# A hybrid attention, delta-rule and linear-attention trunk: the scan's chain gets PSUM banks of its own, and a step's output is normed and gated behind the next step

## The chip, the cores and the metric

The kernel runs on one core of a Trainium2 chip. The metric is the device time of one execution in microseconds (us), as the median of several runs. The engines are TensorE (PE: matmuls, and transposes as matmuls with an identity; PEld is its weight load), VectorE (DVE), ScalarE (ACT), GpSimd (POOL) and SyncE (SP), which issues the DMAs. Each engine works through its instructions in a fixed order. The matmuls' results land in PSUM, which the kernel divides into banks of 128 x 512 float32.

## The reference

Two layers of one trunk over 768 tokens (256 context, 512 latent), model width 1024. In a layer one input projection feeds three groups of heads, whose outputs go through one output projection; a gated ConvFFN follows. Norms and modulation stand around both halves. The core of the first half:

```python
parts = split(norm_and_modulate(x) @ w_in)
mla = softmax((q_nope @ k_nope.T + q_rope @ k_rope.T) * scale) @ v     # 8 heads
# gated delta rule, forward and reversed, 4 heads, chunks of 64 tokens:
v_new = u_ - w_ @ S                      # u_ = Tinv @ (v*beta), w_ = Tinv @ (k*beta*exp(gc))
o     = (q*exp(gc)) @ S + A @ v_new
S     = S * glast + kend.T @ v_new
gdn   = headnorm(o_forward + o_reversed) * gate
gla   = gated linear attention, both directions, headnorm, gate       # 4 heads, chunks of 16 in the reference
x     = x + g * norm(concat(mla, gdn, gla) @ w_out)
x     = x + g * norm(ffn(norm_and_modulate(x)))
```

Only `v_new` and the update of `S` are a chain from chunk to chunk; `o` and everything behind it hang off that chain. All values are float32; large products are made of three fp32r matmuls each (high and low halves).

## The kernel before

The kernel is written with a tile framework. A scheduler fixes each engine's order ahead of time from the order of the program, the tiles that are free and its own estimate of times; on the chip each engine then follows its list. PSUM is one pool: a tag `bb` with two tiles of two banks each, and four tags `a`, `b`, `c`, `d` with one bank and one tile each. `self.ab(tags)` takes the next tag of a string by turns (`"bc"`: b, c, b, c), or of `self.tags` when no string is given. A tag's tiles are handed out in program order: a tile that is asked for later waits until all readers of the tag's tile before it are done.

In a layer, `project_in` makes the input projection: the delta rule's part first, then its preparation for each chunk pair (`gdn_prep`), then `gdn_scan`. The rest of the projection (`rest`) is a generator; `pace` takes 8 pieces of it at two places of each scan step (`SN = (8, 8)`), so that its matmuls stand beside the chain. Behind the scan come `mla_project` (K and Q projections in `bb`, and then six V tiles of 128 x 512, each six matmuls into an `ab()` tile and one ACT copy, L1302), attention for the first of four head pairs, `gla()`, attention for the other three pairs (tags `"ab"`), and the output projection w_out from `mh`, `ml`, the split mixed heads. Attention's tile (128 queries, one head pair): scores in `bb`, L1364 maximum, L1367 exponential into P, transposes of P (bank from `ab()`), copies PT (L1381, L1379), products with V, and L1392, one per tile. Its pool A2 takes the place of the pool A1 in which the K, Q and V projections keep their inputs.

The scan has 12 steps; step n works on chunk n forwards and on a mirrored chunk in reverse, with the two directions on the two halves of the partitions. Before the change a step does, in this order:

- `ks` (tags bc): k·S in columns 0 to 255 and q·S in 256 to 511, 8 matmuls (16 rows in the trace)
- L983 and L984 (DVE): r = v - k·S·eg; then `vp` (bc): tt·r; L995 (DVE): vs, its scaled copy
- `up` twice (bc), one per direction: ktok·vs; POOL L1005 scales the state Sb; L1009 (DVE, four) adds up
- L1013 (DVE): tq = q·S·eg, read from ks; POOL adds the stored output of the other direction (L1015); ACT copies vn
- `op` (bc): at·vn; L1028 (DVE): tq + op, or L1025 into the store `ost` where the other direction comes later
- for n where both directions are there: `head_out`: ACT square (L1058), DVE sum (L1059), square root and reciprocal (L243, L244), POOL scale (L1062), two transposes (L215) into a bc bank, two DVE products with the gate (L1069). Behind every second one a DMA writes the gated output (L1051).

In layer 1 the first four steps need no output (context tokens are dropped there).

Of the kernel before, what the change touches and what calls it, by code (L numbers as in the profile page):

```python
# [11 lines left out]
F32 = mybir.dt.float32  # L12
# [3 lines left out]
ALU = mybir.AluOpType  # L16
# [119 lines left out]
class Net:  # L136
# [40 lines left out]
    def s1(self, pool=None):  # L177
        return (pool or self.B).tile([128, 256], F32, name=self.nm("s"), tag="s", bufs=4 if pool is None else 6)
# [132 lines left out]
    def layer(self, l, later):  # L311
# [32 lines left out]

        with self.ahead(HA):
            self.attention(A2, range(EP[l]))
# [208 lines left out]
    def project_in(self, later):  # L555
# [151 lines left out]
        self.tags = "ad"  # L707
# [249 lines left out]
    def gdn_scan(self):  # L957
# [3 lines left out]
        ost = {}  # L961
# [3 lines left out]
        def s1():  # L965
            return self.s1(self.C)

        for n in range(12):
# [3 lines left out]
            ks = self.ab("bc")  # L972
            for y in range(2 if need_o else 1):
                for d in range(2):
                    c = ch[d]
                    for x in range(2):
                        self.mm(ks[half[d], y * 256 + x * 128:y * 256 + x * 128 + 128],
                                self.KQ[c // 2][:, x, y, half[d]], Sb[:, d, x], True, True)
# [7 lines left out]
            vp = self.ab("bc")  # L986

            for h in range(4):
                for d in range(2):
# [6 lines left out]
                                    self.eks[:, n].unsqueeze(2).to_broadcast(b4), op=ALU.mult)  # L996
            for d in range(2):
                t, hf = ch[d] // 2, ch[d] % 2
                up = self.ab("bc")
# [10 lines left out]
            if need_o:  # L1010
                m = (3 if n < 4 else 15) - n
                vn, tq = s1(), s1()
                nc.vector.tensor_tensor(tq.rearrange(h4, h=4), ks[:, 256:].rearrange(h4, h=4), eg, op=ALU.mult)  # L1013
                if m < n:
                    nc.gpsimd.tensor_tensor(tq, tq, ost[m], op=ALU.add)  # L1015
                nc.scalar.copy(vn, vp[:, :256])
                op = self.ab("bc")
                for h in range(4):
                    for d in range(2):
                        e = d * 4 + h  # L1020
                        self.mm(op[half[d], h * 64:(h + 1) * 64], self.AT[ch[d] // 2][half[d], e * 64:(e + 1) * 64],
                                vn[half[d], h * 64:(h + 1) * 64], True, True)
                if m > n:
                    ost[n] = self.C.tile([128, 256], F32, name=self.nm("ost"), tag="ost", bufs=4)
                    nc.vector.tensor_tensor(ost[n], tq, op[:, :256], op=ALU.add)  # L1025
                    continue

                nc.vector.tensor_tensor(tq, tq, op[:, :256], op=ALU.add)  # L1028
                if n % 2 == 0:
                    lo = min(n, m) - 1  # L1030
                    pieces = [(lo * 64, lo * 64 + 256)] if n < 10 else [(256, 384), (640, 768)]
                    zt = self.gates(0, pieces)
                first = (4 if n >= 10 else lo) if n % 2 == 0 else first
                pos = [c - first if c - first < 4 else c - first - 4 for c in (n, m)]
                self.head_out(tq, zt, [64 * pos[(hf - n) % 2] for hf in range(2)], 0)
                if n % 2:
                    self.ungates(zt, 0, pieces)
# [16 lines left out]
    def head_out(self, o, zt, cols, i):  # L1054
# [8 lines left out]
        ps = self.ab("cd" if i else "bc")  # L1063
# [488 lines left out]
```

## Time and profile before

| | |
|---|---|
| median of 3 runs | 2293.04 us (2292.76 to 2298.89) |
| the profiled execution | 2289.3 us, of them 2287.5 in the span |
| PE busy | 2048.7 us, 90% |
| DVE, ACT, POOL busy | 1306.7 (57%), 1013.0 (44%), 532.2 us (23%) |
| mean granted PE clock | 0.932 of full speed |

Busy times are sums over instructions; a PE at 90% over the span can stand still in one stretch and be full in another. Times in rows count from the span's start. A row's idle time in brackets is how long its engine had nothing to do just ahead of it, with the instruction that ended the wait.

### The profile page before, as it was taken

How to read it: one execution, taken by the hardware profiler on the slowest of the kernel's cores; microseconds unless marked ns; L12 is line 12 of the kernel's file. 1: busy time of each engine (PE TensorE's matmuls, PEld its weight loads, DVE VectorE, ACT ScalarE, POOL GpSimd, SP SyncE). 2: the span in 40 equal slices, each digit the busy share in tenths (PEclk: the TensorE clock that was granted, in tenths of full speed). 3: DMA queues.
4: the chain of work that ended last, by engine and by line, in shares of the span. 5: the costliest groups of instructions: out<-in, count | busy, mean ns of one | idle time of the engine just before them, and what ended most of it. 6: DMA issues, size and time to landing. Idle time of an engine off the chain costs nothing. (4 is left out here: it accounts for less than half of the span.)

```text
span 2287.5 us, 44608 instructions
## 1 busy us (share of the span) xinstructions
PE 2048.7 (90%) x18168; PEld 1674.6 (73%) x18168; DVE 1306.7 (57%) x2474; ACT 1013.0 (44%) x1931; POOL 532.2 (23%) x897
## 2 busy tenths in 40 slices
PE   6899999888888799999999978899878777999996
PEld 3677877665667578888888767787656667888886
DVE  3454535668745743354454685555767757655556
ACT  4653323565454633332232556534456346543333
POOL 1442121135402310001010245222122513211102
PEclk8899999998889899999999978999988888999997
DMA  7233345422043354521222332122412042332332
GB/s 261 66 118 102 107 152 163 139 65 72 8 150 94 125 173 161 166 102 56 65 65 67 99 111 83 51 63 93 151 36 96 6 170 95 110 100 93 101 93 92
DMA packets 121998, 235.64 MB, mean 103 GB/s; under 512 B 9088, under 2 KB 74048, under 8 KB 121792
## 3 DMA queue, kind: packets, MB, share of 16 engines
q1 hardware_dynamic: 121792, 232.78, 31.0%
q8 instruction: 143, 2.34, 0.4%
q14 instruction: 63, 0.52, 0.1%
HBM read 204.04 MB, written 28.70 MB: 102 GB/s over the span
## 5 line engine op out<-in xcount | busy, mean ns | idle before, releaser
L212 PE MATMUL bb<-hh,wl 128*128 128x512 f32 (+1 forms) x1520 | 549.9, 362 | 17.8 <-DVE wl L192 8.4
L212 PE MATMUL bb<-hl,wh 128*128 128x512 f32 (+1 forms) x1520 | 545.8, 359 | 8.1 <-POOL hl L552 6.3
L192 DVE TENSOR_TENSOR wl<-wr,wh 128x512 fp32r<-128x512 f32 (+2 forms) x452 | 336.7, 747 | 365.6 <-ACT wh L191 364.1
L212 PE MATMUL bb<-hh,wh 128*128 128x512 f32 (+1 forms) x1520 | 541.5, 356 | 1.6 <-issue 1.6
L191 ACT CAST wh<-wr 128x512 fp32r<-128x512 f32 (+2 forms) x452 | 274.4, 612 | 525.1 <-PE bb L212 366.2
L212 PEld LDWEIGHTS bb<-hh,wl 128*128 128x128 f32 x1520 | 294.5, 194 | 74.5 <-DVE wl L192 11.7
L212 PEld LDWEIGHTS bb<-hl,wh 128*128 128x128 f32 x1520 | 294.6, 194 | 53.8 <-POOL hl L552 10.5
L212 PEld LDWEIGHTS bb<-hh,wh 128*128 128x128 f32 x1520 | 294.5, 194 | 41.4 <-issue 4.1
L212 PE MATMUL bb<-g,wh 128*128 128x512 f32 (+1 forms) x1024 | 263.6, 349 | 2.3 <-DVE g L192 2.3
L1428 POOL TENSOR_SCALAR y<-u,fmt 128x512 f32<-128x512 f32 (+2 forms) x88 | 80.7, 917 | 528.2 <-ACT u L811 526.7
L212 PEld LDWEIGHTS bb<-g,wh 128*128 128x128 f32 x1024 | 181.6, 195 | 27.5 <-DVE g L192 3.3
L212 PE MATMUL bb<-g,wl 128*128 128x512 f32 (+1 forms) x512 | 180.3, 354 | 21.5 <-DVE wl L192 8.5
L212 PEld LDWEIGHTS bb<-g,wl 128*128 128x128 f32 x512 | 99.3, 195 | 37.0 <-ACT g L191 9.3
L811 ACT ACTIVATE u<-bb,fmt 128x512 f32<-128x512 f32 (+1 forms) x118 | 69.0, 613 | 85.7 <-PE bb L212 85.7
L212 PE MATMUL bb<-mh,wl 128*128 128x256 f32 (+1 forms) x256 | 85.4, 334 | 23.1 <-DVE wl L192 15.5
L1455 DVE TENSOR_TENSOR y<-y,bb 128x512 f32<-128x512 f32 (+2 forms) x80 | 54.7, 685 | 82.4 <-PE bb L212 82.1
L507 POOL TENSOR_TENSOR acc<-acc,sq 128x256 f32<-128x256 f32 (+1 forms) x48 | 49.4, 1029 | 187.6 <-ACT sq L505 186.9
L1429 DVE SCALAR_TENSOR_TENSOR y<-u,fmt,y 128x512 f32<-128x512 f32 (+2 forms) x88 | 72.3, 821 | 29.9 <-POOL y L1428 29.9
L212 PE MATMUL bb<-ml,wh 128*128 128x256 f32 (+1 forms) x256 | 84.1, 328 | 0.3
L1367 ACT ACTIVATE P<-bb,ast,srq 128x768 f32<-128x768 f32 (+1 forms) x80 | 72.6, 908 | 25.4 <-DVE ast L1365 15.6
L212 PE MATMUL bb<-mh,wh 128*128 128x256 f32 (+1 forms) x256 | 82.9, 324 | 0.0
L1364 DVE TENSOR_REDUCE ast<-bb 128x1 f32<-128x768 f32 (+1 forms) x80 | 67.3, 843 | 19.3 <-PE bb L212 18.8
(509 smaller groups left out, 3670.6 us busy)
## 6 DMA issues: line engine op xcount, KB each, us to landing
wr<-in_ffn_w_in SPq DMA_DIRECT2D x92, 512.0 KB, 3.5
wr<-in_w_ada SPq DMA_DIRECT2D x80, 512.0 KB, 4.2
wr<-in_ffn_w_out SPq DMA_DIRECT2D x48, 512.0 KB, 3.5
wr<-in_w_in SPq DMA_DIRECT2D x40, 512.0 KB, 4.0
wr<-in_w_out SPq DMA_DIRECT2D x32, 512.0 KB, 3.6
aw<-in_w_ada SPq DMA_DIRECT2D x16, 512.0 KB, 8.9
x<-in_xT SPq DMA_DIRECT2D x16, 384.0 KB, 8.2
wr<-in_w_uq SPq DMA_DIRECT2D x16, 192.0 KB, 2.5
```

Source lines behind the costliest of these rows:

```text
L191: self.nc.scalar.copy(hi, src)
L192: (eng or self.nc.vector).tensor_tensor(lo, src, hi.bitcast(F32), op=ALU.subtract)
L212: self.nc.tensor.matmul(out, l, r, start=start, stop=stop)
L507: (nc.vector, nc.gpsimd)[k % 2].tensor_tensor(acc[k % 2], acc[k % 2], sq, op=ALU.add)
L811: nc.scalar.activation(u[:, a + o:b + o], ps[:, off + a:off + b], AF.Identity, bias=bias)
L1364: nc.vector.reduce_max(st[:, 0:1], sc, axis=AX)
L1367: nc.scalar.activation(P[:, :w], sc, AF.Exp, bias=st[:, 0:1], scale=self.srq[:, t:t + 1], accum_out=st[:, 1:2])
L1428: nc.gpsimd.tensor_scalar(yv, u[:, lo + 1:lo + 1 + n], cw[1], self.fm(P_FCB + i), op0=ALU.mult, op1=ALU.add)
L1429: nc.vector.scalar_tensor_tensor(yv, u[:, lo:lo + n], cw[0], yv, op0=ALU.mult, op1=ALU.add)
L1455: nc.vector.tensor_tensor(y, y, p, op=ALU.add)
```

## The change

The scan's tags become fixed: `ks` takes b and holds k·S alone, `op` takes d and holds q·S in its upper columns and at·vn in the lower, `vp` takes c, `up` takes b and c. The heads' transposes take a. So that a belongs to what is no part of the chain, the fill of `project_in` and everything behind it until attention takes `"a"` alone instead of `"ad"`; attention sets `"ad"` again. L1013 (tq) now reads `op` behind at·vn; the POOL add of `ost` comes behind the DVE add. `head_out` and the DMA behind it are collected in `late` and emitted behind the next step's output. The pool of [128, 256] tiles `s` in the scan has 8 instead of 6.

```diff
--- before.py
+++ after.py
@@ -175,7 +175,7 @@
         return self.B.tile([128, 512], F32, name=self.nm("h"), tag="h", bufs=HB)
 
     def s1(self, pool=None):
-        return (pool or self.B).tile([128, 256], F32, name=self.nm("s"), tag="s", bufs=4 if pool is None else 6)
+        return (pool or self.B).tile([128, 256], F32, name=self.nm("s"), tag="s", bufs=4 if pool is None else 8)
 
     def bb(self):
         return self.ps.tile([128, 1024], F32, name=self.nm("bb"), tag="bb", bufs=2)
@@ -342,6 +342,7 @@
         self.close(A1p)
         A2p, A2 = self.pool("A2")
 
+        self.tags = "ad"
         with self.ahead(HA):
             self.attention(A2, range(EP[l]))
         with self.ahead(HG):
@@ -704,7 +705,7 @@
         for g in before:
             drain(g)
         self.fill = [rest]
-        self.tags = "ad"
+        self.tags = "a"
         self.gdn_scan()
         self.fill = []
         drain(rest)
@@ -965,17 +966,29 @@
         def s1():
             return self.s1(self.C)
 
+        late = []
+
+        def output(n, tq, zt, cols, last):
+            def go():
+                self.head_out(tq, zt[0], cols, 0)
+                if last:
+                    self.ungates(*zt)
+            return go
+
         for n in range(12):
             ch = (n, self.rstep(n))
             need_o = not (last and n < 4)
             half = [slice(64 * (c % 2), 64 * (c % 2) + 64) for c in ch]
-            ks = self.ab("bc")
-            for y in range(2 if need_o else 1):
-                for d in range(2):
-                    c = ch[d]
-                    for x in range(2):
-                        self.mm(ks[half[d], y * 256 + x * 128:y * 256 + x * 128 + 128],
-                                self.KQ[c // 2][:, x, y, half[d]], Sb[:, d, x], True, True)
+
+            ks = self.ab("b")
+            op = self.ab("d") if need_o else None
+            for y, z in ((0, ks), (1, op)):
+                if z is None:
+                    continue
+                for x in range(2):
+                    for d in range(2):
+                        self.mm(z[half[d], y * 256 + x * 128:y * 256 + x * 128 + 128],
+                                self.KQ[ch[d] // 2][:, x, y, half[d]], Sb[:, d, x], True, True)
             eg = self.egs[:, n].unsqueeze(2).to_broadcast(b4)
             r, v = s1(), s1()
             for d in range(2):
@@ -983,7 +996,7 @@
             nc.vector.tensor_tensor(r.rearrange(h4, h=4), ks[:, :256].rearrange(h4, h=4), eg, op=ALU.mult)
             nc.vector.tensor_tensor(r, v, r, op=ALU.subtract)
             self.pace(SN[0])
-            vp = self.ab("bc")
+            vp = self.ab("c")
 
             for h in range(4):
                 for d in range(2):
@@ -994,9 +1007,12 @@
             vs = s1()
             nc.vector.tensor_tensor(vs.rearrange(h4, h=4), vp[:, :256].rearrange(h4, h=4),
                                     self.eks[:, n].unsqueeze(2).to_broadcast(b4), op=ALU.mult)
+            if need_o:
+                vn, tq = s1(), s1()
+                nc.scalar.copy(vn, vp[:, :256])
             for d in range(2):
                 t, hf = ch[d] // 2, ch[d] % 2
-                up = self.ab("bc")
+                up = self.ab("bc"[d])
                 for h in range(4):
                     x, h2 = h // 2, h % 2
                     self.mm(up[64 * h2:64 * h2 + 64, x * 64:x * 64 + 64], self.ktok[half[d], t, h * 64:(h + 1) * 64],
@@ -1009,32 +1025,32 @@
                     nc.vector.tensor_tensor(o, o, up[ps, :128].rearrange("p (x j) -> p x j", x=2), op=ALU.add)
             if need_o:
                 m = (3 if n < 4 else 15) - n
-                vn, tq = s1(), s1()
-                nc.vector.tensor_tensor(tq.rearrange(h4, h=4), ks[:, 256:].rearrange(h4, h=4), eg, op=ALU.mult)
-                if m < n:
-                    nc.gpsimd.tensor_tensor(tq, tq, ost[m], op=ALU.add)
-                nc.scalar.copy(vn, vp[:, :256])
-                op = self.ab("bc")
                 for h in range(4):
                     for d in range(2):
                         e = d * 4 + h
                         self.mm(op[half[d], h * 64:(h + 1) * 64], self.AT[ch[d] // 2][half[d], e * 64:(e + 1) * 64],
                                 vn[half[d], h * 64:(h + 1) * 64], True, True)
+                nc.vector.tensor_tensor(tq.rearrange(h4, h=4), op[:, 256:].rearrange(h4, h=4), eg, op=ALU.mult)
                 if m > n:
                     ost[n] = self.C.tile([128, 256], F32, name=self.nm("ost"), tag="ost", bufs=4)
                     nc.vector.tensor_tensor(ost[n], tq, op[:, :256], op=ALU.add)
-                    continue
-
-                nc.vector.tensor_tensor(tq, tq, op[:, :256], op=ALU.add)
+                else:
+
+                    nc.vector.tensor_tensor(tq, tq, op[:, :256], op=ALU.add)
+                    nc.gpsimd.tensor_tensor(tq, tq, ost[m], op=ALU.add)
+            for go in late:
+                go()
+            late = []
+            if need_o and m < n:
                 if n % 2 == 0:
                     lo = min(n, m) - 1
                     pieces = [(lo * 64, lo * 64 + 256)] if n < 10 else [(256, 384), (640, 768)]
-                    zt = self.gates(0, pieces)
-                first = (4 if n >= 10 else lo) if n % 2 == 0 else first
+                    zt = (self.gates(0, pieces), 0, pieces)
+                    first = 4 if n >= 10 else lo
                 pos = [c - first if c - first < 4 else c - first - 4 for c in (n, m)]
-                self.head_out(tq, zt, [64 * pos[(hf - n) % 2] for hf in range(2)], 0)
-                if n % 2:
-                    self.ungates(zt, 0, pieces)
+                late.append(output(n, tq, zt, [64 * pos[(hf - n) % 2] for hf in range(2)], n % 2))
+        for go in late:
+            go()
 
     def gates(self, i, pieces):
 
@@ -1060,7 +1076,7 @@
         self.rsqrt(ss, ss, 1.0 / 64, self.eps[:, 0:1])
         ov = o.rearrange("p (h j) -> p h j", h=4)
         nc.gpsimd.tensor_tensor(ov, ov, ss.unsqueeze(2).to_broadcast([128, 4, 64]), op=ALU.mult)
-        ps = self.ab("cd" if i else "bc")
+        ps = self.ab("cd" if i else "a")
         for x in range(2):
             self.transpose(ps[:, x * 128:(x + 1) * 128], o[:, x * 128:(x + 1) * 128])
         pv = ps[:, :256].rearrange("p (x c) -> p x c", x=2)
```

How the orders differ. Names end in the number of the tile.

PE, layer 1, the scan's last steps, before: `c_16817` is vp, `b_16828` ks, `d_17627` and `a_17647` are attention's transposes, `bb_17701` its scores.

```order
L212 MATMUL c_16817<-s_16813,at_15545 64x64
L212 MATMUL c_16817<-s_16813,at_15896 64x64
L212 MATMUL b_16828<-Sb_16220,kq_15884 64x128 x2
L212 MATMUL b_16828<-Sb_16220,kq_15533 64x128 x2
L212 MATMUL b_16828<-Sb_16220,kq_15884 64x128 x2
L212 MATMUL b_16828<-Sb_16220,kq_15533 64x128 x2
L215 MATMUL d_17627<-cst,P_17615 128x128 x2
L215 MATMUL a_17647<-cst,P_17641 128x128 x4
L212 MATMUL bb_17701<-K_2871_17442,Q01l_17463 128x512
L212 MATMUL bb_17701<-K_2871_17442,Q01l_17463 128x256
```

In the place of one head pair's tile there now stands the next step; after, in the place of the step that follows vp `c_16972` (`a_16951` are the transposes of a head, `b_16986` and `c_16994` up, `d_16957` op):

```order
L212 MATMUL c_16972<-s_16966,tt_15498 64x64
L212 MATMUL c_16972<-s_16966,tt_15148 64x64
L215 MATMUL a_16951<-cst,s_16856 128x128 x2
L212 MATMUL b_16986<-s_16981,ktok_13578 64x64 x4
L212 MATMUL c_16994<-s_16981,ktok_13578 64x64 x4
L212 MATMUL d_16957<-s_16983,at_15195 64x64
L212 MATMUL d_16957<-s_16983,at_14842 64x64
```

Attention's rows have gone from between the steps; from step 6 to 11 PE has nothing but the scan's own matmuls and the heads' transposes.

PE, layer 1, V, before: `d_17476` and `a_17485` are the first two V tiles, `c_16683` and `b_16691` one step's up.

```order
L212 MATMUL bb_17561<-K_2871_17442,Q01h_17462 128x256
L212 MATMUL d_17476<-wh_17468,kvl_17138 128x512
L212 MATMUL a_17485<-wh_17468,kvl_17138 128x512
L212 MATMUL c_16683<-s_16681,ktok_13578 64x64 x4
L212 MATMUL b_16691<-s_16681,ktok_13578 64x64 x4
L212 MATMUL d_17476<-wl_17469,kvh_17136 128x512
L212 MATMUL d_17476<-wh_17468,kvh_17136 128x512
L212 MATMUL d_17476<-wh_17472,kvl_17139 128x512
L212 MATMUL a_17485<-wl_17469,kvh_17136 128x512
```

After: `d_17030` is the last step's op, `a_17093` and `a_17105` are the last two heads' transposes, `a_17476` and `a_17485` the first two V tiles.

```order
L212 MATMUL d_17030<-s_17056,at_15195 64x64
L212 MATMUL d_17030<-s_17056,at_14842 64x64
L215 MATMUL a_17093<-cst,s_16984 128x128 x2
L215 MATMUL a_17105<-cst,s_17057 128x128 x2
L212 MATMUL a_17476<-wh_17468,kvl_17138 128x512
L212 MATMUL a_17476<-wl_17469,kvh_17136 128x512
L212 MATMUL a_17476<-wh_17468,kvh_17136 128x512
L212 MATMUL a_17476<-wh_17472,kvl_17139 128x512
L212 MATMUL a_17476<-wl_17473,kvh_17137 128x512
L212 MATMUL a_17476<-wh_17472,kvh_17137 128x512
```

The V tiles, which stood among the scan's steps 6 and 7 in two banks by turns, now stand behind the scan and its last head, in one bank.

PE, layer 0, one of the scan's last three steps, before: `a_5115` and `d_5124` are V tiles, `b_4465` and `c_4473` the step's up.

```order
L212 MATMUL a_5115<-wl_5085,kvh_4677 128x512
L212 MATMUL a_5115<-wh_5084,kvh_4677 128x512
L212 MATMUL b_4465<-s_4463,ktok_453 64x64 x4
L212 MATMUL c_4473<-s_4463,ktok_453 64x64 x4
L212 MATMUL d_5124<-wh_5080,kvl_4678 128x512
L212 MATMUL d_5124<-wl_5081,kvh_4676 128x512
```

After, the last step of layer 0: `bb_5027` is the last Q projection, `b_4599` and `c_4607` are up, `d_4570` is op.

```order
L212 MATMUL bb_5027<-cql_4675,wh_5023 128x256
L212 MATMUL bb_5027<-cqh_4672,wh_5023 128x256
L212 MATMUL b_4599<-s_4594,ktok_453 64x64 x4
L212 MATMUL c_4607<-s_4594,ktok_453 64x64 x4
L212 MATMUL d_4570<-s_4596,at_2146 64x64
L212 MATMUL d_4570<-s_4596,at_1788 64x64
```

The last steps have moved ahead of V and attention's transposes, to the end of the Q projections.

## Rows read from the trace of the kernel before

**Rows 1.** The page: span, and busy time, share and instructions of TensorE.
```profile
span 2287.5 us, 44608 instructions
...
PE 2048.7 (90%) x18168; PEld 1674.6 (73%) x18168; DVE 1306.7 (57%) x2474; ACT 1013.0 (44%) x1931; POOL 532.2 (23%) x897
```

**Rows 2.** Busy us of each engine by stretch, granted clock, DMA share, GB/s.
```profile
254.00:437.00 183.00, 171.81 (x1903) 139.58 (x1904) 89.89 (x206) 61.31 (x120) 33.00 (x40) 0.96 0.46 146
...
437.00:492.00 55.00, 44.40 (x389) 33.73 (x388) 37.42 (x97) 39.80 (x75) 12.43 (x25) 0.91 0.20 61
...
1541.00:1632.00 91.00, 83.64 (x1113) 66.27 (x1104) 58.51 (x120) 34.47 (x68) 19.17 (x26) 0.96 0.43 140
...
1632.00:1646.00 14.00, 12.81 (x120) 9.39 (x119) 6.78 (x18) 7.70 (x15) 1.39 (x2) 1.00 0.24 88
...
1692.00:1718.00 26.00, 15.90 (x167) 11.71 (x166) 10.24 (x33) 10.11 (x19) 5.27 (x8) 0.61 0.04 14
...
1718.00:1758.00 40.00, 36.55 (x350) 27.88 (x350) 27.69 (x74) 26.33 (x57) 9.41 (x23) 0.95 0.40 136
...
1758.00:1823.00 65.00, 51.99 (x608) 39.68 (x608) 50.75 (x102) 27.10 (x52) 36.85 (x42) 0.82 0.02 5
...
1823.00:1846.00 23.00, 10.74 (x137) 6.54 (x137) 9.07 (x29) 7.81 (x20) 2.45 (x4) 0.82 0.19 61
```

**Rows 3.** L995 (DVE, one per scan step) by stretch: busy, count, clock.
```profile
437.00:492.00 55.00, 0.84 (x2) 0.91 0.20 61
...
1541.00:1632.00 91.00, 2.52 (x6) 0.96 0.43 140
...
1692.00:1718.00 26.00, 0.85 (x2) 0.61 0.04 14
```

**Rows 4.** Timeline 1698 to 1709: start, us, engine, instruction, count, [idle before <-releaser].
```profile
1698.30 1.12 PE L212 MATMUL c<-s,tt 64*64 64x64 f32 x16 [0.67 <-DVE zt L1069]
...
1699.46 0.42 DVE L995 TENSOR_TENSOR s<-c,eks 128x256 f32<-128x256 f32 x1 [1.30 <-PE c L212]
...
1700.27 0.37 PE L212 MATMUL b<-s,ktok 64*64 64x64 f32 x2 [0.85 <-DVE s L1013]
...
1701.69 0.59 DVE L1009 TENSOR_TENSOR Sb<-Sb,c 64x128 f32<-64x128 f32 x2
...
1703.51 2.03 PE L212 MATMUL b<-Sb,kq 128*64 128x128 f32 x16 [0.58 <-DVE s L1028]
...
1706.03 0.47 DVE L984 TENSOR_TENSOR s<-s,s 128x256 f32<-128x256 f32 x1
...
1707.03 0.69 PE L215 MATMUL c<-cst,s 128*128 128x128 f32 x2 [1.50 <-POOL s L1062]
...
1708.39 1.12 PE L212 MATMUL c<-s,tt 64*64 64x64 f32 x16 [0.67 <-DVE zt L1069]
```

**Rows 5.** Timeline, PE at 1637: the same products at full clock.
```profile
1637.12 1.15 PE L212 MATMUL b<-Sb,kq 128*64 128x128 f32 x16
```

**Rows 6.** Timeline, ACT, 1644 to 1648: last V copy, table, first P.
```profile
1644.81 0.69 ACT L1302 ACTIVATE V<-a,rr 128x512 f32<-128x512 f32 x1 [0.62 <-PE a L212]
...
1645.51 1.28 ACT L1367 ACT_TABLE_LOAD   x1
...
1646.81 0.99 ACT L1367 ACTIVATE P<-bb,ast,srq 128x768 f32<-128x768 f32 x1
```

**Rows 7.** Timeline, PE: GLA's first transposes, w_out's first matmul.
```profile
1742.97 0.44 PE L215 MATMUL c<-cst,h 128*128 128x128 f32 x2
...
1845.47 0.58 PE L212 MATMUL bb<-mh,wl 128*128 128x256 f32 x1 [6.46 <-ACT mh L191]
```

**Rows 8.** L1392 (DVE, one per attention tile) by stretch.
```profile
437.00:492.00 55.00, 1.44 (x5) 0.91 0.20 61
...
1718.00:1758.00 40.00, 1.42 (x5) 0.95 0.40 136
...
1758.00:1823.00 65.00, 1.69 (x6) 0.82 0.02 5
```

## The prediction

> **What bounds the kernel now.** I read the page first, then busy times by stretch, then a timeline of the barest place of the scan, then waits. TensorE (PE) is busy 2048.7 of 2287.5 us [rows 1], so a change that only reorders work can gain no more than the PE's idle time in the two stretches that it touches. Those are layer 0 from 254 to about 655 us and layer 1 from 1541 to w_out's first matmul at 1845.47 [rows 2, 7]; the orders of before and after are the same on every engine elsewhere. Within them the idle lies unevenly. In 254:437 the scan runs beside the rest of the input projection and the K and Q projections, and PE is busy 171.81 of 183 us; in 1541:1632 it is 83.64 of 91. So ten of twelve scan steps in layer 0 (the other two stand in 437:492) and six in layer 1 [rows 3] are well covered, and a shorter chain there gives at most 11 and 7 us. The weak places are later: in 1692:1718 PE is busy 15.90 of 26 us at a granted clock of 0.61, and in 1823:1846 it is 10.74 of 23 [rows 2]. The first holds the last two scan steps [rows 3], with next to no attention beside them; the second holds the end of GLA, and w_out waits there 6.46 us for the split of the last head's output [rows 7].
>
> **What a step costs, before.** The two last steps show it without cover [rows 4]. From one vp to the next (tt times r, which gives the new values) it is 1708.39 - 1698.30 = 10.1 us at low clock. After vp comes L995 (ends 1699.88); up waits for L1013, the DVE instruction that scales the q part of the bank which up takes over (1700.27, idle 0.85); the state is added up by 1702.28; then ks doesn't start, because the attention-matrix product (at times vn) and its reader L1028 come first in the two shared banks; it starts at 1703.51, after 0.58 of waiting for L1028. ks runs to 1705.54, L984 to 1706.50. vp could follow at about 1706.6, but its bank belongs to the head's transposes, which wait 1.50 us for POOL (L1062), and to their reader L1069: 1708.39. So the shared banks cost 0.34 + 1.2 + 1.8 = 3.4 us of the 10.1.
>
> **The change, part by part.** *Banks.* k·S goes to b and q·S to d with at·vn, so up waits for L995 alone and ks for the state alone. Then vp to up is 1.12 + 0.04 + 0.42 + 0.06 = 1.64; up to ks is 1702.28 - 1700.27 + 0.06 = 2.07; ks to vp is 3.1 in the rows (1703.51 to 1706.6). Of its ks, only the k half (1.0 of 2.03 us) must be done before L983, so 2.1. The sum is 5.8 us at low clock, and by the ratio 1.15 to 2.03 of the same ks [rows 4, 5] about 1 us less at full clock. at·vn and the q half fall into the waits for DVE. I take 5.5. Bounds: 4.6, and 8 if the head's DVE and POOL instructions, which stand in the same queues, cut in as often as now.
> *Late output.* The twelve heads' instructions are the same; each is issued a step later. It costs nothing where a next step covers it; behind the last step nothing does. L1059, L1062 (1.50 wait seen by PE), two transposes and L1069 are then bare: from L1028's end, just ahead of ks, to vp's start behind L1069, 1708.39 - 1703.45, about 5 us [rows 4]; I take 5, and 6 with the copy of the last tile.
> *More s tiles, the add of ost behind the DVE add.* No instruction is added. Eight tiles instead of six only free a wait; the POOL add moves between at·vn and the head, off the chain: 0 (bound: one POOL add per step, inside those 5 us).
> *Tags.* This is the part that moves work. project_in's fill, the heads' transposes and the V tiles all take bank a alone, and tiles of one bank are served in program order. V's six tiles are emitted behind the scan, so they cannot start before the last head's transposes. Before, V alternated d and a and could pass the scan's last steps. And attention's first P waits for V's copies (its pool lies where the projection's tiles lay): before, the last V copy ended at 1645.50 and P starts at 1646.81, after the 1.3 us in which ACT loads its table [rows 6]. So attention can't start before the scan is over. The order shows just that: six steps directly behind each other in layer 1, then two heads' transposes, then V.
>
> **Layer 1, summed.** Step 5's vp I put at 1633, as before, where its L995 is the last of six ahead of 1632 [rows 3]: nothing ahead of it moves by more than the 7 idle us of that stretch. Six steps and the rest of this one: 6.6 x 5.5 = 36, to 1669. The last head: 5 to 6, to 1675. V: in d and a by turns the six tiles and one step's work fit into the 14 us of 1632:1646, 12.81 of them busy [rows 2], so a tile has 1.6 us of PE (without the step's 3.0) to 2.3; in one bank each also shows its copy, 0.69 [rows 6], and two starts, so 14 to 20, taken 17: 1692. Table load and P, 1.3 + 0.99 and their starts: 1695, where before had 1648 [rows 6]. From here attention has PE to itself. A tile's pace: five tiles in the 40 us of 1718:1758 [rows 2, 8] is 8.0 us, with GLA's loads and first matmuls already in it, so 7.6 to 8.0, taken 7.8; w_out starts beside the last tile, so 15.7 tiles are 122 us. GLA's own price: before, 1718 to 1846 held 11 tiles [rows 2, 8], 128 - 11 x 8.0 = 40 is the upper bound; the lower is from PE's work alone, 36.55 + 51.99 + 10.74 = 99.3 less 11 x 7.3 (36.55 / 5) = 19. I take 30: GLA starts as soon as the scan has ended (its first transposes stood at 1742.97 [rows 7], 35 us behind the scan's last vp, and will stand beside V) and so mixes with all of attention, but not perfectly. 1695 + 122 + 30 = 1847, against 1845.5: **+1.5**, with -11 (7.6 and 19) and +14 (8.0 and 40) as bounds. In words: the bare 26 us and the tail of 23 us are given back, and a start of attention that is 47 us later is paid for it.
>
> **Layer 0, summed.** Three of the twelve steps stood beside V and attention (two of them in 437:492 [rows 3]); now they come ahead. Of PE's work a step has ks 1.15, vp and at·vn 0.64 each (1.12 by the clock's ratio) and up about 0.5: 3.0 us, so +9 in a stretch where PE idles only 11.2 of 183 us [rows 2]. V in one bank +5, the last head +4, P's start +1.5, and +2 where the fill waits in bank a behind a head's transposes: 21.5. Given back: 437:492 held 5 tiles' ends [rows 8] and two steps in 55 us; without the steps 55 - 5 x 8 = 15 at most, the steps' PE work of 9 at least, taken 11. And of the 11.2 idle us, 7 by a chain that waits less. **+3.5**, bounds -4 and +12.
>
> The sum is +5 on the profiled execution's 2289.3 us. The median of the runs is 2293.04, 3.7 above it, and the runs spread over 6; between 2294 and 2298 I say **2296 us**. That is 0.13% over the median, inside the 0.3% (6.9 us) that a measurement can tell from no change.
>
> **What the rules say.** The six V tiles took d and a in turn and PE was busy 12.81 of 14 us with them and one step [rows 2]. The Trainium skill (Perfetto Trace Analysis, Matmuls) says that independent groups should rotate through different PSUM banks, so that one's evacuation lies beside the next one's matmuls. By that rule alone this part of the change loses some 4 to 6 us in each layer, an estimate, which is what the rows gave above; no row of before has V in one bank. And in 1692:1718 the granted clock is 0.61, between its levels of 1.2 and 2.4 GHz, in the stretch in which PE waits most [rows 2]. The same skill (TensorE: Matmul & The Clock Gate, HAM oscillation) says that idle gaps which come back in each round of a loop throttle the engine again and again. This is the rival C below.
>
> **Rivals.** *B, faster (0.28).* GLA and attention overlap well: PE-bound pace 7.3 and a price of 19 give 1695 + 115 + 19 = 1829, -16; layer 0 with +2 makes -14: about 2279. For it: GLA ends as the very last now, with 12.3 idle us in 23, and starts some 50 us earlier relative to attention after. Against it: in 1758:1823, where both were at work, PE was busy only 51.99 of 65 at clock 0.82 [rows 2].
> *C, slower (0.25).* The bare steps don't shrink: the norm's chain over ACT, DVE and POOL cuts into the chain of the state, and PE waits at low clock as now. At 8 us a step layer 1 loses 6.6 x 2.5 = 16 more; with layer 0's +6 it comes to about +23: 2316. It decides from 6.5 us a step on (+7 us). For it: six such steps in a row instead of two, at 0.61. Against it: three waits in [rows 4] go by construction.
> *D, no effect (0.07).* The cover hides both: PE is busy 94% of 254:437, and in layer 1 the order is overruled by GLA's chain: 2293.
>
> **Chances.** The forecast has 0.40, its own range 2288 to 2304; D is in it. Faster: B 0.28 and 0.03 of the forecast's edge, 0.31. Slower: C 0.25 and 0.09 of the upper edge, 0.34. Same: 0.35. The range takes in B and most of C: 2272 to 2316.
>
> **What would show it.** In layer 1's timeline after: six vp at 5 to 6 us from each other (right) or at 8 and more (C); V's copies all behind the last head's transposes, in one bank, some 2.5 to 3 us apart; the first P near 1695; GLA's last transposes before the last attention tile's end; w_out near 1847 with no 6 us idle ahead. In layer 0, no scan instruction among attention's, and w_out some 3 us later. Wrong would be a first P before 1680 or after 1705, or attention tiles at over 9 us with GLA's work spread among them.

## The result, and the profile after

The changed kernel took 2313.9 us (median of 6 runs, 2308.15 to 2322.89) against 2292.9 for the kernel before (6 runs, 2287.19 to 2298.89): a ratio of 1.0099, with a 95% interval of 1.0076 to 1.0122. It is slower by about 1%. Its profiled execution took 2308.7 us, 19.4 above that of before.

The page of the kernel after, its span and TensorE's row, which answer to [rows 1]:

```profile
span 2307.0 us, 44590 instructions
...
PE 2056.0 (89%) x18168; PEld 1674.4 (73%) x18168; DVE 1314.4 (57%) x2474; ACT 1008.1 (44%) x1927; POOL 534.9 (23%) x897
```

PE's busy time rose by 7 us, the span by 19.5. Four points in each trace part the span: the first step's vs (L995, after L1008), w_out's last matmul in layer 0, a matmul b<-kq of layer 1's preparation of the scan (at 1501.9 before, at 1517.3 after), and w_out's last in layer 1. All times are us; starts of instructions:

| | before | after | difference |
|---|---|---|---|
| first vs | 265.6 | 265.9 | |
| layer 0: to w_out's last matmul | 479.5 | 494.1 | +14.6 |
| between: to layer 1's preparation (nearly the same order) | 756.7 | 757.4 | +0.7 |
| layer 1: to w_out's last matmul | 407.1 | 408.7 | +1.6 |

The loss is layer 0's. Layer 1 came out nearly even, as forecast. Busy us by stretch after (columns as in [rows 2]):

```profile
254.00:436.00 182.00, 172.30 (x1933) 136.24 (x1932) 90.03 (x212) 55.89 (x115) 36.03 (x46) 0.95 0.42 135
...
436.00:472.50 36.50, 24.08 (x104) 15.03 (x103) 15.19 (x39) 10.84 (x24) 8.85 (x15) 0.63 0.36 122
...
472.50:683.00 210.50, 179.49 (x1722) 135.73 (x1722) 152.07 (x367) 128.06 (x260) 79.04 (x110) 0.90 0.21 73
...
1651.00:1683.00 32.00, 24.30 (x399) 17.83 (x399) 22.52 (x65) 9.71 (x25) 10.79 (x17) 0.95 0.04 12
...
1683.00:1690.20 7.20, 2.25 (x30) 1.31 (x28) 3.88 (x14) 1.24 (x4) 1.91 (x3) 0.75 0.11 36
...
1690.20:1714.50 24.30, 13.97 (x54) 9.04 (x54) 2.38 (x7) 7.44 (x15) 2.21 (x6) 0.79 0.26 82
```

The first stretch ends with the last Q projection (before: 420.3), the second with attention's first transposes (before: 436.8), the third with the last attention tile (before: 660.4). The 36.5 us of the second had 16.5 before; PE is busy 24.08 of them, at a granted clock of 0.63. In layer 1 the six bare steps take 1651:1683, then the last heads and V another 31.5 us.

One bare step after, timeline, which answers to [rows 4]:

```profile
1670.84 0.68 PE L212 MATMUL c<-s,tt 64*64 64x64 f32 x16 [0.41 <-DVE s L997]
...
1671.57 0.42 DVE L1008 TENSOR_TENSOR s<-c,eks 128x256 f32<-128x256 f32 x1 [0.78 <-PE c L212]
...
1672.05 0.45 PE L212 MATMUL b<-s,ktok 64*64 64x64 f32 x8 [0.53 <-DVE s L1008]
...
1673.23 0.58 DVE L1025 TENSOR_TENSOR Sb<-Sb,c 64x128 f32<-64x128 f32 x2
...
1673.96 0.62 PE L212 MATMUL b<-Sb,kq 128*64 128x128 f32 x6 [0.18 <-DVE Sb L1025]
...
1674.84 0.42 DVE L996 TENSOR_TENSOR s<-b,egs 128x256 f32<-128x256 f32 x1
...
1675.29 0.78 DVE L997 TENSOR_TENSOR s<-s,s 128x256 f32<-128x256 f32 x1
...
1676.13 0.68 PE L212 MATMUL c<-s,tt 64*64 64x64 f32 x16 [0.40 <-DVE s L997]
```

From vp to vp it is 5.3 us instead of 10.1, and up waits for L1008 alone. All six steps together: L1008 stood at 1651.6 and 1682.1, 30.5 us or 5.1 each, at a clock of 0.95 where before had 0.61. The rows that answer to [rows 7]:

```profile
1704.53 0.63 PE L215 MATMUL c<-cst,h 128*128 128x128 f32 x2
```

```profile
1865.30 0.39 PE L212 MATMUL bb<-mh,wl 128*128 128x256 f32 x1
```

GLA's first transposes stand 38 us earlier in a layer that began 15.5 us later, and w_out no longer waits behind GLA.

What PE waited for between the last Q projection and attention's first transposes in layer 0, the kernel after (engine, what, line, releaser: us in total, times, longest):

```profile
PE a L215 <- POOL s L1078: 3.9, 2, 2.5
...
PE a L212 <- ACT V L1318: 3.2, 5, 0.8
...
PE c L215 <- POOL h L1142: 2.1, 1, 2.1
...
PE a L215 <- ACT P L1383: 1.8, 1, 1.8
...
PE a L212 <- DVE zt L1085: 0.7, 1, 0.7
```

Two heads' transposes wait 3.9 us for POOL and V for the second one's readers; each V tile waits for the copy of the one ahead; and GLA's transposes, which the scan's early end has brought in between V tiles, wait 2.1 us for POOL with V behind them.

### The profile page after: what moved, and what is told of

The parts are those of the page before. It is cut to its first block, busy times and chain, and to the rows that moved or that the text cites. A ratio compares the mean times of both kernels' runs of the same rounds, so it can differ in the third digit from the quotient of the medians.

```text
span 2307.0 us, 44590 instructions
## 1 busy us (share of the span) xinstructions
PE 2056.0 (89%) x18168; PEld 1674.4 (73%) x18168; DVE 1314.4 (57%) x2474; ACT 1008.1 (44%) x1927; POOL 534.9 (23%) x897
## 4 chain that ended last, share of the span: by engine, by line
PE 69%; DVE 13%; ACT 6%; DMA 6%; issue 4%; POOL 1%; SPq 1%; DVEq 0%; ACTq 0%; POOLq 0%
PE bb L212 54%; PE a L212 4%; PE c L212 3%; PE d L212 3%; PE b L212 3%; DVE y L534 2%; DMA wr<-in_w_in 1%; DVE wl L192 1%; PE a L215 1%; ACT P L1383 1%; DMA aw<-in_w_ada 1%; DVE ast L1380 1%; ACT wh L191 1%; DVE x L535 1%; ACT PT L1397 0%
## 5 line engine op out<-in xcount | busy, mean ns | idle before, releaser
L212 PE MATMUL bb<-g,wh 128*128 128x512 f32 (+1 forms) x1024 | 265.6, 351 | 2.3 <-DVE g L192 2.3
L508 POOL TENSOR_TENSOR acc<-acc,sq 128x256 f32<-128x256 f32 (+1 forms) x48 | 49.4, 1029 | 176.4 <-ACT sq L506 176.0
```

What stands on the lines that cost most here:

```text
L212: self.nc.tensor.matmul(out, l, r, start=start, stop=stop)
L508: (nc.vector, nc.gpsimd)[k % 2].tensor_tensor(acc[k % 2], acc[k % 2], sq, op=ALU.add)
```

## The experiments

All times below are medians beside the kernel before in the same batch (2290.5 to 2292.9); the ratio and its interval are against that kernel. "Layer 0" takes in the stretch between, since the point that parts the two moves by some us from one execution to the next; both are differences to the profile of before, and single profiles: 5 us say nothing. (From the first b<-kq matmul of layer 1's preparation to the last Q matmul the changed kernel took 176.4 us and heads at once 182.3, with one and the same order on DVE and ACT up to the scan.)

| | median | ratio (95%) | layer 0 | layer 1 |
|---|---|---|---|---|
| changed kernel | 2313.9 | 1.0099 (1.0076 to 1.0122) | +15.3 | +1.6 |
| V in a and d | 2290.25 | 1.0000 (0.9976 to 1.0024) | +8.5 | -10.1 |
| V in c alone | 2293.78 | 1.0009 (0.9988 to 1.0030) | +8.4 | -9.7 |
| V in b, c, d | 2268.03 | 0.9903 (0.9875 to 0.9931) | -5.1 | -18.0 |
| V in b, c, d in layer 0 alone | 2290.66 | 0.9982 (0.9964 to 1.0001) | -4.4 | -5.0 |
| V in b, c, d, heads at once | 2281.09 | 0.9943 (0.9923 to 0.9964) | -2.6 | -11.1 |
| heads at once | 2308.95 | 1.0073 (1.0044 to 1.0101) | +14.3 | +6.8 |
| heads in d | 2282.60 | 0.9964 (0.9951 to 0.9978) | -5.6 | -4.0 |
| heads in d, attention in a | 2297.05 | 1.0044 (1.0023 to 1.0065) | +7.9 | -10.4 |
| V in b, c, d, attention in a, b, d | 2277.79 | 0.9948 (0.9930 to 0.9965) | -8.3 | -8.2 |
| before, late output, 8 s tiles | 2277.66 | 0.9925 (0.9903 to 0.9948) | -2.8 | -12.4 |
| before, late output, 6 s tiles | 2280.08 | 0.9954 (0.9938 to 0.9970) | -0.9 | -11.8 |
| before, V in a alone | 2288.44 | 0.9989 (0.9969 to 1.0010) | -0.4 | +7.0 |

**V's banks.** Theory T: what the change lost is V, which stands in bank a behind the last heads and goes through one bank; rival R: the scan's steps ahead of attention. The edit is one line in `mla_project` ("ad" here, "bcd" and "c" in the next two; `"a" if l else "bcd"` where layer 0 alone is changed):

```diff
         self.V = []
+        self.tags = "ad"
         wh, wl = self.wsplit(self.a["w_uv"][l])
```

> The changed kernel, but the six V tiles of each layer take d and a by turns, as before, instead of a alone. The order on every engine stays that of the changed kernel outside V. Theory T (what the change lost is V: its tiles wait in bank a for the last heads' transposes and then go one by one, and attention's first P waits for them): the first V tile no longer waits for the last heads, V ends some 14 us earlier in layer 0 (456 to 460 instead of 471.7) and some 11 earlier in layer 1; in all 15 to 24 us below the changed kernel, about 2285 to 2294 in its profile. Rival R (the scan's steps that stand ahead of attention are the price, with the low clock around them; V's banks only decide where PE waits): within 5 us of the changed kernel, 2304 to 2309.

> The changed kernel, but the V tiles take b, c and d by turns, the scan's banks, which are free behind the last step; the heads' transposes keep a. V then waits for no head at all. Theory T: V starts right behind the last step's products and ends some 20 us earlier in layer 0 and some 15 earlier in layer 1 than in the changed kernel; 22 to 32 us below it, about 2277 to 2287, below the kernel before. Rival R: 2302 to 2309, within 6 of the changed kernel.

Measured: 2290.25 and 2268.03, T in both, the second by 9 us more than it asked for; R asked for 2302 to 2309. From the last Q matmul to attention's first transposes layer 0 takes 36.6 us after, 23.2 with a and d, and 16.4 with b, c and d (before: 16.7), in each case with all twelve steps ahead. In layer 1, from the last L1008 to attention's first transposes, it is 32.4, 19.7 and 13.7 us. The profiles of the changed kernel and of the version with b, c and d are 40.4 us apart; these two stretches make 20.2 and 18.7 of it.

With a and d V's tiles do not take turns on PE: three tiles in d go ahead of and beside the heads' transposes, and then three in a. So this edit too takes V from behind the heads, and no run gives V a second bank with the heads still ahead of it. Two V tiles and the heads in this version:

```profile
444.18 0.47 PE L212 MATMUL d<-wh,kvl 128*128 128x512 f32 x1 [0.96 <-DVE s L1039]
...
445.73 0.44 PE L215 MATMUL a<-cst,s 128*128 128x128 f32 x2
...
448.08 0.38 PE L215 MATMUL a<-cst,s 128*128 128x128 f32 x2
...
450.51 0.39 PE L212 MATMUL a<-wh,kvl 128*128 128x512 f32 x1
```

That all twelve steps stand ahead is no loss by itself: with b, c and d the last Q matmul starts 171.0 us behind the first vs instead of 154.5, and layer 0 is not longer. Windows of the version with b, c and d, last Q to first transposes in layer 0, last step to first transposes in layer 1:

```profile
440.60:457.00 16.40, 12.88 (x87) 10.10 (x86) 8.88 (x24) 8.62 (x17) 1.96 (x3) 1.00 0.47 161
...
1667.00:1679.20 12.20, 9.26 (x51) 7.34 (x45) 3.60 (x14) 7.23 (x13) 1.92 (x3) 1.00 0.15 45
```

Nothing is left of the wait for the heads: 12.88 of 16.40 us busy at full clock.

> The changed kernel with V's six tiles in c alone: still one bank and one tile after another, but not behind the heads' transposes in a. It parts the two halves of V's price. In layer 0 the changed kernel had V's first matmul 10.6 us behind the last Q projection and the last copy 24.2 us behind that; with b, c and d these were 4.6 and 8.7. If the wait for the heads is the larger half: V is over within some 14 us of its start, and the time is 2270 to 2285. If the single bank is: V takes 18 to 24 us from an earlier start, 6 us a layer are gained, 2293 to 2301. The first V tiles' copies may also stand behind GLA's first activations on ACT, as in the changed kernel, which goes with the second.

Measured: 2293.78, at the lower edge of "the single bank is the larger". The stretches say the other. Without the heads ahead the 36.6 us of layer 0 fall by 15.0 (to 21.6), and three banks instead of one take another 5.2 (to 16.4). In layer 1 32.4 us fall by 14.0 (to 18.4) and then by 4.7 (to 13.7). So the wait for the heads is the larger half in both layers, and V in c took 15.5 us from its first matmul to its last copy, near the 14 of that theory and not 18 to 24.

The time is longer than that theory's for a reason that I had overlooked: the edit also moved the scheduler's order of DVE, ACT and POOL in layer 1's preparation, far from V. From the preparation's first b<-kq matmul to the last Q matmul this kernel took 185.9 us, the changed kernel and the version with b, c and d, whose orders there are the same, 176.4. The moved order also stands in V in a and d (183.2), in heads in d with attention in a (180.0) and in attention in a, b, d (182.7). So the times of these four hold some 4 to 9 us that are not the price of what they were to test; that is an estimate from single profiles, of which 5 us may be chance.

The same stretch of this kernel:

```profile
436.50:458.00 21.50, 14.41 (x86) 9.58 (x84) 11.14 (x33) 8.53 (x17) 4.81 (x10) 1.00 0.62 206
```

Its V tiles go through one bank, as in the changed kernel, at a clock of 1.00. V's matmuls alone, in the kernel after and in this one:

```profile
446.60:470.80 24.20, 18.80 (x54) 11.58 (x54) 6.51 (x16) 6.93 (x13) 6.90 (x12) 0.50 0.26 88
```

```profile
440.80:455.10 14.30, 10.52 (x42) 6.68 (x40) 4.23 (x14) 5.62 (x9) 3.77 (x9) 1.00 0.59 194
```

Two of V's matmuls in the kernel after, and two in that with b, c and d:

```profile
447.15 0.63 PE L212 MATMUL a<-wl,kvh 128*128 128x512 f32 x1
...
447.57 0.63 PE L212 MATMUL a<-wh,kvh 128*128 128x512 f32 x1
```

```profile
445.39 0.40 PE L212 MATMUL b<-wl,kvh 128*128 128x512 f32 x1
...
445.62 0.39 PE L212 MATMUL b<-wh,kvh 128*128 128x512 f32 x1
```

From start to start it is 0.43 us after and 0.23 there. For 36 matmuls that is 7 us, most of the 8.7 us by which V is shorter in c alone (from its first matmul to the start of its last copy 440.8 to 456.3, against 446.6 to 470.8); the wait of 2.1 us for GLA's transposes is in the rest. So the wait for the last heads costs twice in layer 0: PE idles in it, and V behind it runs at the low clock. The second price differs: in layer 1 of the same execution V behind the heads had 0.78, and in the three other stretches in which V stands behind the heads (layer 1 with b, c, d in layer 0 alone, both layers with heads at once) 0.80 and 0.82. In both layers with a and d, with c alone and with b, c and d it had 1.00.

In the Trainium skill (TensorE: Matmul & The Clock Gate, HAM oscillation) idle gaps that come back in each round of a loop throttle the engine again and again. These stretches are not parted by gaps that come back: V in a and V in c both have gaps of up to 0.8 us ahead of their tiles, at 0.50 and 1.00, and the six bare steps, where I had expected the low clock, kept 0.95 with gaps of 0.1 to 0.5 us in each round.

> The changed kernel with V in b, c and d by turns in layer 0 alone; layer 1 as in the changed kernel. By the traces the layers' shares of what this brought were 13 to 15 us in layer 0 and 19 in layer 1: 13 to 18 us below the changed kernel, 2290 to 2296, if the two are independent. If layer 0 alone made it all, about 2270; if layer 1, 2305 to 2309.

Measured: 2290.66. The time is in the range, which I had counted from the changed kernel's profile; from its median it is 23.2 us, more than the 13 to 18. The other 22.6 us of the medians come with layer 1. No run has layer 1 alone, so whether the two are independent is not shown. Its layer 1, which keeps V in a and nearly all of the changed kernel's order, came out 6.6 us shorter than in that kernel's profile. One wait in it makes some 4 of that. ACT and DVE in the changed kernel:

```profile
1693.20 0.69 ACT L1318 ACTIVATE V<-a,rr 128x512 f32<-128x512 f32 x1 [5.74 <-PE a L212]
...
1693.90 1.28 ACT L1124 ACT_TABLE_LOAD   x1
...
1700.03 0.69 DVE L1121 TENSOR_TENSOR_SCAN h<-h,h 128x256 f32<-128x256 f32 x1 [9.92 <-DMA h<-sp]
...
1700.97 0.20 ACT L1124 ACTIVATE glgl<-gtot 128x4 f32<-128x4 f32 x1 [5.78 <-DVE gtot L1123]
...
1701.08 0.67 ACT L1318 ACTIVATE V<-a,rr 128x512 f32<-128x512 f32 x1
```

GLA's first activation (L1124) stands between V's copies, since GLA too starts when the scan ends. It waited 5.8 us for a DMA's data by way of DVE, and the copy and PE's next V tile behind it. In this experiment the same wait is short (waits of ACT):

```profile
ACT glgl L1124 <- DVE gtot L1123: 1.6, 1, 1.6
```

**The late output and the heads.**

```diff
-            for go in late:
-                go()
-            late = []
             if need_o and m < n:
...
                 late.append(output(n, tq, zt, [64 * pos[(hf - n) % 2] for hf in range(2)], n % 2))
-        for go in late:
-            go()
+                for go in late:
+                    go()
+                late = []
```

> The changed kernel with its banks and tags, but a step's output norm and gate are emitted at once, as before, and not behind the next step. Theory T (the late output costs little, V's bank costs nearly all): within 8 us of the changed kernel, since V still stands in bank a behind the last head; the bare steps of layer 1 grow from 5.0 us to 6 or 7 with the norm's DVE work in their queue, about 2305 to 2318. Rival R2 (the late output is what loses, since it leaves two heads behind the last step): 2293 to 2301.

> V in b, c and d by turns, banks of the change, but the output's norm and gate emitted at once instead of behind the next step. With V free of the heads this prices the late output by itself: the three bare steps of layer 1 that have a head behind them took 7.1, 8.4 and 7.0 us with heads at once and 5.2 with late ones, so 6 us more in layer 1 and nothing in layer 0: 4 to 9 us above V in b, c and d with late output, 2270 to 2280. If late output only mattered through V, the same within 3 us.

Measured: 2308.95, as theory T had it, and 2281.09. With V in a the place of the output is lost in V's wait: the intervals of the two kernels overlap. With V free, output at once costs 9 us by the two ratios (13 by the medians of two batches; the intervals just overlap), the upper edge of the 4 to 9 that I expected; the time lies 1.1 us above its range. Layer 1 in the profiles has 6.9 of it. Starts of the last four vp, output at once, then late:

```profile
1649.39 0.68 PE L212 MATMUL c<-s,tt 64*64 64x64 f32 x16
...
1655.95 0.68 PE L212 MATMUL c<-s,tt 64*64 64x64 f32 x16 [1.87 <-DVE s L997]
...
1664.44 1.12 PE L212 MATMUL c<-s,tt 64*64 64x64 f32 x16 [1.63 <-DVE s L997]
...
1671.92 0.68 PE L212 MATMUL c<-s,tt 64*64 64x64 f32 x16 [1.63 <-DVE s L997]
```

```profile
1649.16 0.68 PE L212 MATMUL c<-s,tt 64*64 64x64 f32 x16
...
1654.25 0.68 PE L212 MATMUL c<-s,tt 64*64 64x64 f32 x16 [0.40 <-DVE s L997]
...
1659.61 0.68 PE L212 MATMUL c<-s,tt 64*64 64x64 f32 x16
...
1664.84 0.68 PE L212 MATMUL c<-s,tt 64*64 64x64 f32 x16 [0.34 <-DVE s L997]
```

Steps of 6.6, 8.5 and 7.5 us against 5.1 to 5.4: the norm's DVE and ACT instructions in the chain's queues, which rival C had feared of the late output, are there when it is not late.

On the old banks:

```diff
+            for go in late:
+                go()
+            late = []
+            if need_o and m < n:
...
-                self.head_out(tq, zt, [64 * pos[(hf - n) % 2] for hf in range(2)], 0)
-                if n % 2:
-                    self.ungates(zt, 0, pieces)
+                late.append(output(tq, zt, [64 * pos[(hf - n) % 2] for hf in range(2)], n % 2, pieces))
+        for go in late:
+            go()
```

> The kernel before with the late output alone: a step's norm and gate are emitted behind the next step, with 8 s tiles; banks and tags as before (ks, vp, up, op and the heads' transposes in b and c by turns, V and attention in a and d). If the late output is worth something without banks of its own, the vp of the last steps no longer waits for a head's transposes; 2 to 8 us below before in its profile. If the shared banks keep the chain bound, within 3 us of before. A theory by which the late output itself is what loses expects 8 or more above before.

> The kernel before with the late output alone, and with 6 s tiles as before instead of 8. It tells whether the 15 us that late output with 8 tiles brought on the old banks come from the later place of the norm or from two more tiles. If from the place: 2272 to 2283. If from the tiles: 2288 to 2296, as before.

Measured: 2277.66 and 2280.08. I had expected 2 to 8 us and got 15 and 12, and it is the place, not the two tiles, that makes nearly all of it. Layer 1 makes 12 of it. The last three steps take 34.3 us from vs to vs instead of 42.9, and GLA, which ended layer 1 before, starts earlier. The issue of GLA's first load (start, us, queue, line), before and with the late output:

```profile
1728.24 0.42 SPq L1093 DMA_DIRECT2D h<-gkd  x1
```

```profile
1721.26 0.42 SPq L1105 DMA_DIRECT2D h<-gkd  x1
```

Counted from each layer's preparation (1501.9 and 1504.3) that is 9.4 us earlier.

The kernel before with `self.tags = "a"` ahead of V and `"ad"` ahead of attention:

> The kernel before with one change: V's six tiles take a alone (attention a and d as before). V still isn't behind the heads and can pass the scan's steps, which fill the gaps that each copy leaves. Theory T (V loses because it stands behind the last heads with nothing beside it; the one bank comes on top): 1 to 5 us above before, since steps stand in the gaps. Rival R3 (the one bank alone makes V's loss of 13 us that the changed kernel shows in layer 0): 10 us or more above before.

Measured: 2288.44, no difference to before that can be told, and R3 is out: one bank costs the kernel nothing where the scan's steps stand in V's gaps, though V itself takes 14.9 and 18.1 us in the two layers of its profile instead of 11.0 and 12.0. (Its profiled execution, the slowest of its ten, lies above that, so its layers in the table are not used.)

> The changed kernel, but the heads' transposes take bank d, which they share with op, and leave a to the fill and V. V is then not behind the heads and stands among the last steps of the scan in both layers, still in one bank. Theory T: attention starts some 12 us earlier than in the changed kernel in layer 0 and is no later in layer 1; 10 to 25 us below the changed kernel, about 2284 to 2299. Rival R (the steps ahead of attention are the price): the order of the steps in layer 0 has two of them behind V again, so 5 to 8 below, 2300 to 2304. If heads and op in one bank slow the chain, the steps in layer 1 go from 5.0 us to over 6.

```diff
-        ps = self.ab("cd" if i else "a")
+        ps = self.ab("cd" if i else "d")
```

Measured: 2282.60, 1.4 us below the range of T. V passes the heads and the scan's last steps, and layer 0 is as short as with b, c and d. In layer 1's order the first pair's attention waits behind op and the heads in d for the scan's end, and less is gained.

Two more edits change `self.tags = "ad"` ahead of attention: to `"a"` with the heads in d, and to `"abd"` with V in b, c and d.

> The heads' transposes in d beside op, V and the first head pair's attention in a alone. The scan then holds b, c, d and nothing that stands behind it in program order, so that V and attention can pass it in both layers, as before, and the chain still has banks of its own. If the scan's cover is worth more than a second bank for attention: below V in b, c and d, 2255 to 2268. If one bank slows attention's tiles (8 to over 10 us each for ten tiles in two layers): 2275 to 2295.

> V in b, c and d by turns, and attention's first head pair takes a, b and d by turns instead of a and d. In the version with V in b, c and d PE waited in layer 0 some 10 us for L1409 (the last reader of an attention tile's bank), and 10 for P and PT. If banks bound the first pair's attention: 2 to 8 us below V in b, c and d, 2258 to 2266. If ACT and DVE bound it: the same within 3 us.

Measured: 2297.05 and 2277.79, misses both. With attention's first pair in a alone layer 0 is 13 us longer than with a and d. With a third bank for it the time is 10 us over V in b, c and d, not under; attention's last tile of layer 1 ended 346 us behind the layer's preparation, not 334, while GLA ended earlier. The moved order in layer 1's preparation (180.0 and 182.7 us against 176.4) is in both times. Why a third bank turns attention and GLA round is open.

## Why the prediction was right or wrong

The time lies in the range; the forecast, no change that can be told, was wrong, and the kernel is slower by 1%. That the range holds it is in part luck: it reaches up to rival C's 2316, and C is not what happened.

- **A step without cover.** Right: 5.5 us taken, 5.1 measured. Rival C's steps of 8 us and its low clock are not there.
- **Layer 1.** Forecast +1.5 to w_out's first matmul; measured +4.4 to that and +1.6 to its last, both counted from the preparation and inside the bounds. (These bounds, -11 and +14, come out as -12 and +15 from their own terms.) Inside, the last head and V took 32.4 us from the last L1008 to attention's transposes, forecast some 28; the six steps were 2.5 us shorter, and attention with GLA took 150.8 us, forecast 152. GLA's earlier start did pay for attention's later one.
- **Layer 0.** Forecast +3.5, measured +14.6. The step that failed is in "V in one bank +5, the last head +4, P's start +1.5". Those 10.5 us were 19.9 (36.6 against 16.7). The term for the one bank was right: with V free of the heads, one bank against three is 5.2 us. The last head, priced at +4, was the wrong one: V behind the heads against V in c alone is 15.0 us. I had priced the head as a wait alone and V behind it at full clock. V's first matmul came 10.6 us behind the last Q matmul instead of 4.5, V behind it ran at the low clock, and GLA's first instructions came in between. The other terms were each off and cancelled: the last Q matmul came 15.5 us later, not 4 (PE's idle time ahead of it rose from 8.8 to 9.7 us instead of falling by 7; 9 us of it are the three steps, the other 6 are not taken apart), and from attention's first transposes to w_out's end 20.9 us were given back, not 11. Their net is -5.4, forecast -7.
- **The orders elsewhere.** I had called them the same. Around 1360 to 1400 us some instructions of ACT, DVE and POOL stand at other places; the stretch between the layers' parts came out at +0.7 us.
- **The rule of the banks.** The Trainium skill (Perfetto Trace Analysis, Matmuls) says that independent groups should rotate through different PSUM banks. I weighed that at 4 to 6 us a layer. With V free of the heads, one bank against three is 5.2 us in layer 0 and 4.7 in layer 1, so the weight was right; in the kernel before, with steps in the gaps, one bank costs nothing that can be told. What a second bank is worth with the heads still ahead, no run shows.
- **The late output.** I gave it no value. Alone, on the old banks, it brings 12 to 15 us, and about 9 on top of the new banks with V free.

So the change is two gains and a tag that gave back more than both. The new banks with V in b, c and d and heads at once stand at a ratio of 0.9943, in which V's three banks are counted too; the late output alone at 0.9925 and 0.9954; both together at 0.9903, and its interval overlaps with the first of the two, so what the banks add to the late output is small and not well known. The tag costs some 45 us: V in bank a, in line behind the last heads, one tile at a time, and attention behind V. With V in b, c and d, which the scan has left by then, the change makes the kernel 1% faster than before.

## What to carry to other kernels

When a chain gets resources of its own, look at what is pushed together in those that are left: tiles of one tag are served in program order, so a tag that is shared by the chain's epilogue and the next stage's prologue puts one behind the other, whatever the scheduler could have done. Give the next stage the chain's own banks, which are free exactly then. Price a wait ahead of dense work also at a lower clock behind it, which it can leave. And when an edit is to test one thing, compare the engines' orders far from it as well: a scheduler can move them.

## What the runs showed of the hardware

In layer 0 V's matmuls behind waits of 2.5 and 1.4 us for the heads ran at a granted clock of 0.50, the lower of its two levels (1.2 GHz). In layer 1 of the same execution, behind waits of 3.0 and 1.4 us, the mean was 0.78. V in c alone, without these waits ahead of it but with the same gaps of up to 0.8 us ahead of its tiles, ran at 1.00 in both layers. Over the six bare scan steps, with gaps of 0.1 to 0.5 us, the clock was 0.95, although PE was busy only 24.30 of their 32 us. I had expected the low clock in these.
